# Row normalisation on one core: every load and store as one DMA with one descriptor per partition

## The chip, the cores and the metric

One Trainium2 chip, of which one core runs the program. The core has compute engines (DVE, the vector engine; ACT, the scalar engine; POOL; PE, the matrix engine, unused here), a synchronisation engine SP that here issues loads, and 16 DMA engines that move data between HBM, where the inputs and outputs lie, and the on-chip memory of 128 partitions. The metric is the device time of one execution in microseconds, lower is better.

## The reference

```python
def setup_inputs():
    batch, seq, dim = 32, 512, 1024
    return {"x": np.random.randn(batch, seq, dim).astype(np.float32)}

def reference(x):
    sums = np.sum(np.abs(x), axis=-1, keepdims=True)
    return (x / (sums + 1e-8)).astype(np.float32)
```

Each of the 16,384 rows of 1,024 float32 values is divided by the sum of its absolute values. 67.11 MB are read and 67.11 MB written.

## The kernel before

The 16,384 rows are dealt out to 128 partitions, 128 rows to each, and cut into 11 tiles: ten of 12 rows per partition (48 KB per partition, 6,144 KB in all) and a last one of 8 rows (32 KB per partition, 4,096 KB in all). `piece` says which rows of HBM a tile stands for. Tiles 0, 1 and 10 share a head region of 32 rows per partition, so that in HBM a partition's part of such a tile lies 128 KB from the next partition's; tiles 2 to 9 are contiguous blocks. Within a tile one partition's rows are always one contiguous run in HBM and in the on-chip memory.

Four tile buffers (`BUFS = 4`) hold a tile each, and the result is written over the input in place. The order is written by hand: loads 0 to 3 are issued by SP at the start; then for each tile its compute, its store, and the load of the tile four places on, which goes into the buffer that the store has just emptied. Load i+4 therefore waits on SP until store i has landed in HBM. Loads are issued on SP's DMA queue (q1 in the profile), stores on ACT's (q10); both queues feed the same 16 DMA engines, each of which serves 8 of the 128 partitions.

The compute of a tile (`normalize`): DVE sums the absolute values of all rows in one reduction (L47), adds the epsilon (L54) and takes the reciprocal (L56). The rows are then multiplied: the first `kv` rows by one DVE instruction (L58), the next `kt` rows one by one on DVE (L65), the last ones one by one on ACT (L68). `split` gives `(kt, ks)` by tile; for tile 0 it is `(3, 4)`: five rows in L58, three in L65, four on ACT. For tiles 3 to 8 DVE does all rows in L58.

How a transfer is cut into descriptors is set by `max_dma_last_dim`, the most bytes that one descriptor may move; one descriptor is one packet in the profile's count. `HALF` is 24,576 B, half a partition's part of a full tile, `WHOLE` is 49,152 B, all of it. Loads 0 and 1 go out whole (one descriptor per partition), all later loads in halves (L87); the last load, of 32 KB per partition, becomes two of 16 KB. Store 0 is two DMAs: its first three rows (`FIRST = 3`) in descriptors of one row, 4 KB, then nine rows in one descriptor of 36 KB. Stores 1 to 7 are one DMA with two descriptors per partition; store 8 (`last - 2`) is two DMAs of six rows, 24 KB each; stores 9 and 10 are one DMA with one descriptor per partition (L97).

Of the kernel before, what the change touches and what calls it, by code (L numbers as in the profile page):

```python
# [1 line left out]

# [4 lines left out]

FP32 = mybir.dt.float32
EPS = 1e-8


@with_exitstack
def kernel(
    ctx: ExitStack,
    tc: tile.TileContext,
    x: bass.AP,
    out: bass.AP,
):
    nc = tc.nc
    P = nc.NUM_PARTITIONS  # L20

    x_flat = x.flatten_outer_dims()
    out_flat = out.flatten_outer_dims()
    n, d = x_flat.shape

    R = 12
    BUFS = 4
    HEAD = 32
    per_partition = n // P
    assert n % P == 0 and (per_partition - HEAD) % R == 0  # L30
    rows = [R] * ((per_partition - HEAD) // R + 2) + [HEAD - 2 * R]

    def piece(flat, i):
        head = flat[: P * HEAD, :].rearrange("(p r) d -> p r d", p=P)
        if i < 2:
            return head[:, R * i : R * (i + 1), :]
        if i == len(rows) - 1:
            return head[:, 2 * R :, :]
        a = P * (HEAD + R * (i - 2))
        return flat[a : a + P * R, :].rearrange("(p r) d -> p r d", p=P)  # L40

    sbuf = ctx.enter_context(tc.tile_pool(name="sbuf", bufs=BUFS))
    stats = ctx.enter_context(tc.tile_pool(name="stats", bufs=len(rows)))

    def normalize(x_tile, k, kv, kt):
        s = stats.tile([P, R], FP32)
        nc.vector.tensor_reduce(  # L47
            out=s[:, :k],
            in_=x_tile[:, :k, :],
            axis=mybir.AxisListType.X,  # L50
            op=mybir.AluOpType.add,
            apply_absolute_value=True,
        )
        nc.vector.tensor_scalar_add(out=s[:, :k], in0=s[:, :k], scalar1=EPS)  # L54
        inv = stats.tile([P, R], FP32)
        nc.vector.reciprocal(out=inv[:, :k], in_=s[:, :k])  # L56
        if kv:
            nc.vector.tensor_mul(  # L58
                out=x_tile[:, :kv, :],
                in0=x_tile[:, :kv, :],  # L60
                in1=inv[:, :kv].unsqueeze(2).to_broadcast([P, kv, d]),
            )
        for r in range(kv, kv + kt):
            row = x_tile[:, r, :]
            nc.vector.tensor_scalar_mul(out=row, in0=row, scalar1=inv[:, r : r + 1])  # L65
        for r in range(kv + kt, k):
            row = x_tile[:, r, :]
            nc.scalar.activation(  # L68
                out=row,
                in_=row,  # L70
                func=mybir.ActivationFunctionType.Copy,
                scale=inv[:, r : r + 1],
            )

    last = len(rows) - 1
    split = {0: (3, 4), 1: (0, 3), 2: (0, 3), last - 1: (0, 2), last: (4, 4)}

    tiles = {}

    HALF, WHOLE = 24576, 49152
    FIRST = 3

    def load(i):
        x_tile = tiles[i] = sbuf.tile([P, R, d], FP32, name="x_tile")
        nc.sync.dma_start(out=x_tile[:, : rows[i], :], in_=piece(x_flat, i), max_dma_last_dim=WHOLE if i < 2 else HALF)  # L87

    def store(i):
        if i == 0:  # L90
            parts = [(0, FIRST, 4 * d), (FIRST, R, WHOLE)]
        elif i == last - 2:
            parts = [(0, R // 2, HALF), (R // 2, R, HALF)]
        else:
            parts = [(0, rows[i], WHOLE if i >= last - 1 else HALF)]
        for a, b, size in parts:
            nc.scalar.dma_start(  # L97
                out=piece(out_flat, i)[:, a:b, :],
                in_=tiles[i][:, a:b, :],
                max_dma_last_dim=size,  # L100
            )

    def compute(i):
        k = rows[i]
        kt, ks = split.get(i, (0, 0))
        normalize(tiles[i], k, k - kt - ks, kt)

    with tc.manual_schedule():
        for i in range(BUFS):
            load(i)  # L110
        for i in range(len(rows)):
            compute(i)
            store(i)
            if i + BUFS < len(rows):
                load(i + BUFS)


# [1 line left out]
_INS = ['x']  # L119
_OUTS = [((32, 512, 1024), 'float32')]  # L120


# [23 lines left out]
```

## Time and profile before

| what | value |
|---|---|
| median of 3 runs | 316.5 us (316.41 to 316.51) |
| span of the profiled execution, first to last instruction | 315.2 us |
| time of the profiled execution beyond its span | not given by the profile; the median is 1.3 us above the span |
| HBM read and written | 67.11 MB each, 426 GB/s over the span |
| DVE: reductions (L47), 11 | 138.2 us |
| DVE: broadcast multiplications (L58), 10 | 113.6 us |
| ACT: row multiplications (L68), 16 | 17.2 us |
| DMA issues | 11 loads (SP), 13 stores (ACT) |
| loads of 6,144 KB, issue to landing, median | 36.9 us |
| stores of 6,144 KB, issue to landing, median | 49.1 us |

The span runs from the first to the last instruction. Busy time of an engine is given as time and share of the span; issuing a DMA is not counted as busy time, so the issuing queues appear as SPq and ACTq. A row of instructions ends with the idle time just before it in brackets and what ended it. For DMA queues the profile counts packets, MB and the share of the time of all 16 engines that the packets took. A small packet of 4 bytes that marks the completion of a DMA on an engine is counted as well.

### The profile page before, as it was taken

The numbers are of one execution on the slowest core, as the hardware profiler recorded it, in microseconds if no ns is written. First come the engines' busy times: TensorE is split into PE (matmuls) and PEld (weight loads), VectorE is DVE, ScalarE is ACT, GpSimd is POOL, SyncE is SP. The second block draws the span as 40 slices with busy tenths as digits, with TensorE's granted clock in tenths as the row PEclk, the third lists the DMA queues.
The fourth block names the chain that finished last, engine by engine and source line by source line (L and its number), as shares of the span: only waits on it lengthen the run. The fifth ranks groups of instructions, "written<-read, shape, count | busy, mean of one in ns | idle before, by whom it ended". The sixth has DMA issues, their size and how long they took to land.

```text
span 315.2 us, 172 instructions
## 1 busy us (share of the span) xinstructions
DVE 260.6 (83%) x50; ACT 18.5 (6%) x17; POOL 0.2 (0%) x4
## 2 busy tenths in 40 slices
DVE  0079999999999999989996997999699969999000
ACT  0010503004000000000000000000000000203200
POOL 0000000000000000000000000000000000000000
DMA  8999999999999999999999999999999999999997
GB/s 318 480 399 412 437 407 464 411 436 413 415 446 437 415 446 437 415 449 434 415 449 437 412 449 437 412 449 437 415 446 437 415 437 434 432 428 496 399 408 324
DMA packets 5761, 134.22 MB, mean 426 GB/s; under 512 B 385, under 2 KB 385, under 8 KB 769
## 3 DMA queue, kind: packets, MB, share of 16 engines
q1 hardware_dynamic: 2736, 67.11, 49.8%
q10 hardware_dynamic: 3024, 67.11, 49.4%
q14 instruction: 1, 0.00, 0.0%
HBM read 67.11 MB, written 67.11 MB: 426 GB/s over the span
## 4 chain that ended last, share of the span: by engine, by line
DVE 40%; DMA 33%; another core or an unknown queue 18%; ACT 1%; issue 0%; SPq 0%
DVE s L47 23%; DMA x_tile<-in_x_dram 17%; DMA out_dram<-x_tile 16%; DVE x_tile L58 15%; ACT x_tile L68 1%; DVE x_tile L65 1%; DVE inv L56 0%; DVE s L54 0%; SPq L87 0%
## 5 line engine op out<-in xcount | busy, mean ns | idle before, releaser
L47 DVE TENSOR_REDUCE s<-x_tile 128x12 f32<-128x12288 f32 (+1 forms) x11 | 138.2, 12562 | 29.8 <-DMA x_tile<-in_x_dram 29.8
L58 DVE TENSOR_TENSOR x_tile<-x_tile,inv 128x12288 f32<-128x12288 f32 (+3 forms) x10 | 113.6, 11358 | 0.5
L68 ACT ACTIVATE x_tile<-x_tile,inv 128x1024 f32<-128x1024 f32 x16 | 17.2, 1138 | 256.9 <-DVE inv L56 256.9
L65 DVE TENSOR_SCALAR x_tile<-x_tile,inv 128x1024 f32<-128x1024 f32 x7 | 4.8, 749 | 0.0
L56 DVE RECIPROCAL inv<-s 128x12 f32<-128x12 f32 (+1 forms) x11 | 2.5, 226 | 0.4
L68 ACT ACT_TABLE_LOAD x1 | 1.3, 1283 | 17.8 <-DMA x_tile<-in_x_dram 17.8
L54 DVE TENSOR_SCALAR s<-s 128x12 f32<-128x12 f32 (+1 forms) x11 | 1.9, 174 | 0.4
L130 POOL MEMSET const-bfloat16-1.0<- 128x1 bf16 x1 | 0.1, 101 | 0.0
L130 POOL MEMSET const-uint8-127<- 128x1 uint8 x1 | 0.1, 101 | 0.0
L130 POOL MEMSET const-float32-0.0<- 128x1 f32 x1 | 0.1, 98 | 0.2 <-issue 0.2
L130 POOL MEMSET const-float32-1.0<- 128x1 f32 x1 | 0.1, 98 | 0.0
## 6 DMA issues: line engine op xcount, KB each, us to landing
x_tile<-in_x_dram SPq DMA_DIRECT2D x10, 6144.0 KB, 36.9
out_dram<-x_tile ACTq DMA_DIRECT2D x8, 6144.0 KB, 49.1
out_dram<-x_tile ACTq DMA_DIRECT2D x2, 3072.0 KB, 33.4
out_dram<-x_tile ACTq DMA_DIRECT2D x1, 4608.0 KB, 37.9
x_tile<-in_x_dram SPq DMA_DIRECT2D x1, 4096.0 KB, 32.2
out_dram<-x_tile ACTq DMA_DIRECT2D x1, 4096.0 KB, 20.9
out_dram<-x_tile ACTq DMA_DIRECT2D x1, 1536.0 KB, 29.3
```

Of the source, the lines that this page charges most:

```text
L47: nc.vector.tensor_reduce(out=s[:, :k], in_=x_tile[:, :k, :], axis=mybir.AxisListType.X, op=mybir.AluOpType.add, apply_absolute_value=True,)
L54: nc.vector.tensor_scalar_add(out=s[:, :k], in0=s[:, :k], scalar1=EPS)
L56: nc.vector.reciprocal(out=inv[:, :k], in_=s[:, :k])
L58: nc.vector.tensor_mul(out=x_tile[:, :kv, :], in0=x_tile[:, :kv, :], in1=inv[:, :kv].unsqueeze(2).to_broadcast([P, kv, d]),)
L65: nc.vector.tensor_scalar_mul(out=row, in0=row, scalar1=inv[:, r : r + 1])
L68: nc.scalar.activation(out=row, in_=row, func=mybir.ActivationFunctionType.Copy, scale=inv[:, r : r + 1],)
L130: nc = _bacc.Bacc("TRN2", target_bir_lowering=False, num_devices=1)
```

## The change

All loads and stores are issued without `max_dma_last_dim`. One partition's part of a tile is a contiguous run, and so each load and each store becomes one DMA with one descriptor per partition: 48 KB for tiles 0 to 9, 32 KB for tile 10. Store 0 is no longer cut into its first three rows and the rest, and store 8 no longer into two halves. The compute, the four buffers, the order of issue and the queues are the same.

```diff
-    HALF, WHOLE = 24576, 49152
-    FIRST = 3
-
     def load(i):
         x_tile = tiles[i] = sbuf.tile([P, R, d], FP32, name="x_tile")
-        nc.sync.dma_start(out=x_tile[:, : rows[i], :], in_=piece(x_flat, i), max_dma_last_dim=WHOLE if i < 2 else HALF)
+        nc.sync.dma_start(out=x_tile[:, : rows[i], :], in_=piece(x_flat, i))
 
     def store(i):
-        if i == 0:
-            parts = [(0, FIRST, 4 * d), (FIRST, R, WHOLE)]
-        elif i == last - 2:
-            parts = [(0, R // 2, HALF), (R // 2, R, HALF)]
-        else:
-            parts = [(0, rows[i], WHOLE if i >= last - 1 else HALF)]
-        for a, b, size in parts:
-            nc.scalar.dma_start(
-                out=piece(out_flat, i)[:, a:b, :],
-                in_=tiles[i][:, a:b, :],
-                max_dma_last_dim=size,
-            )
+        nc.scalar.dma_start(out=piece(out_flat, i), in_=tiles[i][:, : rows[i], :])
```

## The prediction

> **What bounds the kernel now.** I read the page first: the engine rows, the slices and the queues.
>
> ```profile
> span 315.2 us, 172 instructions
> DVE 260.6 (83%) x50; ACT 18.5 (6%) x17; POOL 0.2 (0%) x4
> ...
> DMA  8999999999999999999999999999999999999997
> ...
> q1 hardware_dynamic: 2736, 67.11, 49.8%
> q10 hardware_dynamic: 3024, 67.11, 49.4%
> ```
>
> The 16 DMA engines are busy in every slice and their two queues together fill 99.2% of the span; DVE, the busiest compute engine, fills 83%. So the end is set by the sum of what the DMA engines must do, unless some order of the work leaves them with nothing to do. q1 carries the loads (issued by SP), q10 the stores (issued by ACT). Next I read the busy time by stretches:
>
> ```profile
> 40.00:50.00 10.00, 10.00 (x1) 0.00 (x0) 0.00 (x0) 1.00 1.00 424
> 50.00:60.00 10.00, 9.90 (x4) 3.23 (x3) 0.00 (x0) 1.00 0.97 414
> ...
> 86.00:96.00 10.00, 10.00 (x1) 0.00 (x0) 0.00 (x0) 1.00 1.00 433
> ...
> 160.00:189.10 29.10, 26.34 (x5) 0.00 (x0) 0.00 (x0) 1.00 1.00 432
> ...
> 289.00:313.30 24.30, 2.70 (x4) 4.22 (x4) 0.00 (x0) 1.00 1.00 432
> ```
>
> The last column is GB/s. The rate is 432 to 433 where loads and stores of 24 KB packets mix and where only stores of 48 and 32 KB are left; it is lower only from 40 to 60 us, where the first store's 4 KB packets run. Third, the DMA view of two stretches, 41 to 62 us (first pair) and 77 to 80 us (last line), packets and MB by queue:
>
> ```profile
> q1 hardware_dynamic: 323, 7.54, 83.7%
> q10 hardware_dynamic: 322, 1.32, 15.2%
> ...
> x_tile<-in_x_dram SPq DMA_DIRECT2D x1, 6144.0 KB, 33.2
> ```
>
> Packets are as many in both queues while bytes stand 6 to 1: an engine takes one packet (one descriptor's record) from each queue in turn, whatever its size. And load 4, issued at 76.8 us into an empty q1, lands after 33.2 us. Fourth, the timeline gives the rhythm and the tail:
>
> ```profile
> 168.21 12.95 DVE L47 TENSOR_REDUCE s<-x_tile 128x12 f32<-128x12288 f32 x1 [2.60 <-DMA x_tile<-in_x_dram]
> ...
> 197.29 12.95 DVE L47 TENSOR_REDUCE s<-x_tile 128x12 f32<-128x12288 f32 x1 [2.62 <-DMA x_tile<-in_x_dram]
> ...
> 279.85 0.34 ACTq L97 DMA_DIRECT2D out_dram<-x_tile  x1
> ...
> 293.25 0.34 ACTq L97 DMA_DIRECT2D out_dram<-x_tile  x1
> ```
>
> Each reduction starts when its load lands, every 29.08 us. In that time an engine moves 16 load and 16 store packets of 24,576 B: 0.909 us each. Load 4 thus came 33.2 - 29.1 = 4.1 us late: about 1.0 us from issue to a first packet (load 0: issue 0.73, first packet record 1.74) and 3.4 packets of the other queue already taken up.
>
> **The packets that go.** Each engine serves 8 of the 128 partitions. Packets per engine before: loads 2 x 8 whole, 8 x 16 half and 16 in the last tile, 160; stores 8 x (3 + 1) for tile 0, 7 x 16, 16 for tile 8, 8 and 8 for the last two, 176. Together 336, and 16 x 336 plus 24 DMAs x 16 completion records is 5760, the page's 2736 + 3024. After: 22 DMAs x 8 = 176. So 160 packets per engine go, the bytes stay. The price of one: in the packet records two starts on one engine lie 908 ns apart for 24,576 B and 1812 ns for 49,152 B; 2 x 908.3 - 1811.8 = 4.8 ns is saved by joining two. 4,096 B take 155 ns, which gives 4.7 ns beside the same rate. 160 x 4.7 ns = 0.75 us. By the recorded durations (912 and 1815 ns, which overlap a little) it is 9 ns and 1.4 us; if joining saved nothing, 0. I take 0.75, since starts on a busy engine are what adds up to the end.
>
> **The first store.** Load 0 lands at 17.8. If the engines then ran at their steady rate, load 1 (8 x 1.812 = 14.5), loads 2 and 3 (32 half packets, 29.1) and store 0 (8 x (3 x 0.155 + 1.360) = 14.6) would be done at 17.8 + 58.2 = 76.0. The second part of store 0, issued at 38.8 (the two issues together last from 36.78 to 39.18), lands 37.9 us later: 76.7. So 0.7 us are lost here, where the table shows 424 and 414; the packet records show it as load packets of up to 1.6 us instead of 0.91 beside 4 KB stores, up to 65 us, and hardly any after that. After the change no 4 KB packet exists and every mix is of large packets. Bounds: 0 (the loss belongs to the first mixing of the queues, whatever the size) and -0.7. The nearest row is the mix of equal large packets (433 and 432 GB/s, no slow packet), so I take -0.7.
>
> Its first rows now wait for the rest of the tile: ACT issues at 38.8 instead of 36.8, behind DVE's three row multiplications. Cost nothing: q1 has loads 2 and 3 queued, so no engine idles; behind it on ACT stands only tile 1's work at 52.1. Two issues (0.4 us each) vanish from ACT, which is idle 256.9 us: nothing. SP's queue is the same 11 issues in the same order, each behind the landing of the store four tiles earlier.
>
> **What moves, and whether it stays covered.** A newly filled queue now waits behind larger packets: 1.0 + 3.4 x 1.812 = 7.2 us. Store 0 begins at 38.8 + 7.2 = 46.0, just as load 2 is through; load 3 and store 0 then alternate 16 packets and both land near 17.8 + 4 x 14.5 = 75.8. Load 4 is issued there, begins at 83.0, and with 15 packets in turn (27.2) and 0.9 to the landing (before: 80.9 + 31 x 0.909 = 109.1, landed 110.0) is there at about 111.1, where DVE comes free (111.2 before). From then on 16 x 1.812 = 28.99 us a tile: load 9 lands at 256.1 (255.5 before), store 9 is issued at 279.85 + 0.6 = 280.5. Load 10 (8 x (1.21 + 1.81) = 24.2) lands at 280.3, store 10 is issued near 294. The engines, meanwhile, are to finish at about 312.3 (their last packet ends at 313.8 before, less the 1.45 us summed below), so store 9's packets begin at 312.3 - 8 x 1.21 - 8 x 1.81 = 288.1 and it has 288.1 - 280.5 - 1.0 = 6.6 us to spare (before: store 9, issued 279.85, landed after 24.6; 304.45 less 14.5 and 0.5 is 289.5, so 8.6). Loads up to 6.6 us later cost nothing; beyond that each microsecond is one at the end.
>
> **Sum.** -0.75 - 0.7 = -1.45 us on a span of 315.2: 313.7. The profile gives no time for its execution beyond the span; the runs' median of 316.5 is 1.3 above it, which I leave as it is: 315.05, given as 315.1 us (-0.45%).
>
> **Rivals.**
> 1. Only packets are saved; the 0.7 us come again where 48 KB stores first meet loads. For it: the slow packets sit at the start and at the end of the first mix. Against: the mixes from 81 us on begin without any. 316.5 - 0.75 = 315.75.
> 2. No change: the saving is eaten or the joint packet is not cheaper in a mix, which no row of 48 KB beside 48 KB shows. 316.5.
> 3. Slower, mixed large packets: a load packet waits for its data when a packet of 48 KB stands before it. A row for such a wait is the 4 KB mix, where a load packet takes 938 ns on average from its start to the next instead of 908. 30 ns on the 64 load packets of tiles 3 to 10 is +1.9 us: 316.5 - 0.75 + 1.9 = 317.65. It outweighs the saving from 12 ns a packet on and is measurably slower from 22. Against it: the 24 KB mix shows none, nor does the last load's mix of 16 KB with 24 KB.
> 4. Slower, the tail runs dry: if a new queue waits for more than 3.4 packets, load 4 and every later load come later, DVE follows, and past 6.6 us (from 7 packets on) the engines idle between stores 8 and 9. At 9 packets load 4 is 5.6 x 1.81 = 10.1 us later than reckoned, 3.5 us past the slack: 318.6; each packet more is 1.8 us more. Against it: 33.2 us for load 4, and 323 packets beside 322. The Trainium skill (DMA: Bandwidth & Descriptors, Queues, rings and completion order) has this rule: an engine drains about 9 to 17 descriptors from one queue before it turns to the next. By that rule the trace does not agree: turns here are of one descriptor, and load 4's 4.1 us leave room for three or four.
>
> **How the numbers follow.** No change means within 0.2%, 315.87 to 317.13, about what a measurement of this kernel can tell. Forecast 0.38, rival 1 0.17, rival 2 0.17, rival 3 0.20, rival 4 0.08. Faster: 0.37 of the forecast and 0.11 of rival 1, 0.48. Same: the rest of these two, 0.07, 0.15 of rival 2 and 0.02 of rival 3, 0.24. Slower: 0.18 of rival 3, 0.08 and 0.02 of rival 2, 0.28. The forecast's own range is 314.4 (the packets at 9 ns) to 315.7. With both signs in play the range of eight in ten goes from 314.4 to 317.9, just past rival 3.
>
> **What would show it.** q1 and q10 with 1584 packets each; reductions 29.0 us apart from tile 5 to 9; store 0 landing near 76 and load 4 about 35 us after its issue; 432 GB/s or more from 45 to 75 us (a dip there is rival 1); a rhythm above 29.1 us is rival 3; a slice with idle DMA after 280 us is rival 4. Store 10 issued at 294 with DMA busy to the end would bear out that the order of loads is covered. The forecast is wrong if the rhythm does not shorten, or if it does and the span does not.

## The result, and the profile after

The change makes the kernel slower, by 0.4%: 317.61 us median (316.97 to 320.25, 13 executions) against 316.58 us (316.38 to 316.73, 13 executions) of the kernel before, ratio 1.0041, 95% interval 1.0025 to 1.0057. It also makes it uneven: before's executions lie within 0.35 us of each other, the changed kernel's within 3.3.

The profiled execution of the changed kernel is one of the shortest, 316.97 us with a span of 315.0. Its page, the engine rows, the slices and the queues:

```profile
span 315.0 us, 168 instructions
DVE 260.5 (83%) x50; ACT 18.5 (6%) x17; POOL 0.2 (0%) x4
...
DMA  8999999999999999999999999999999999999997
...
q1 hardware_dynamic: 1584, 67.11, 49.8%
q10 hardware_dynamic: 1584, 67.11, 49.2%
```

1584 packets in each queue, as the descriptors say, and the DMA engines as busy as before. The timeline, for the rhythm and the two last stores:

```profile
169.17 12.95 DVE L47 TENSOR_REDUCE s<-x_tile 128x12 f32<-128x12288 f32 x1 [2.53 <-DMA x_tile<-in_x_dram]
...
198.17 12.95 DVE L47 TENSOR_REDUCE s<-x_tile 128x12 f32<-128x12288 f32 x1 [2.53 <-DMA x_tile<-in_x_dram]
...
280.53 0.34 ACTq L85 DMA_DIRECT2D out_dram<-x_tile  x1
...
293.82 0.34 ACTq L85 DMA_DIRECT2D out_dram<-x_tile  x1
```

Loads land every 29.00 us (29.08 before). Store 9 is issued at 280.53, store 10 at 293.82. Now the DMA view of two stretches, 38.8 to 46 us (first line) and 120 to 149 us (the pair); columns are packets, MB, share of the time of 16 engines:

```profile
q1 hardware_dynamic: 39, 1.92, 79.3%
...
q1 hardware_dynamic: 144, 6.29, 50.1%
q10 hardware_dynamic: 144, 6.29, 50.1%
```

In the steady mix both queues have 144 packets, 128 of data and 16 small completions: 0.501 x 29 us x 16 / 128 = 1.816 us a packet, the price of 48 KB. From 38.8 to 46 us, where the first store begins, 39 load packets take 0.793 x 7.2 x 16 = 91.4 us, 2.34 us each, on average half a microsecond too much; in the packet records the excess stands in one or two load packets of each engine, where its first store packet comes. The busy time by stretches (last column GB/s) shows the same place:

```profile
40.00:50.00 10.00, 10.00 (x1) 0.00 (x0) 0.00 (x0) 1.00 1.04 393
50.00:60.00 10.00, 9.90 (x4) 3.23 (x3) 0.00 (x0) 1.00 0.99 428
...
160.00:189.10 29.10, 26.41 (x5) 0.00 (x0) 0.00 (x0) 1.00 1.00 434
```

393 GB/s where before had 424. Large packets make a ten-microsecond figure coarse (a packet counts where it starts); added up from the packet records, the time beyond the usual duration is 1.29 us per engine here, all of it between 40 and 47 us. Before it was 0.67 us, and most of it stood elsewhere: 0.1 us from 38 to 50 us, beside the first 4 KB store packets, and over 0.5 us from 62 to 65 us, in the last two packets of load 3. The DMA view of before from 62 to 64.5 us has these 32 load packets:

```profile
q1 hardware_dynamic: 32, 0.79, 95.2%
```

0.952 x 2.5 x 16 / 32 = 1.19 us each instead of 0.91. In the changed kernel no load packet is late there. So one stall has gone, and a larger one has come at another place.

So this execution shows a saving in the mix and a loss at its start. It does not show why the median is 1 us above before. The spans of all executions, which are listed beside their times, say more:

| kernel | spans, us | median | time beyond the span |
|---|---|---|---|
| before, 32 executions beside the later runs | 314.8 to 315.3 | 315.0 | 1.63 |
| changed, the 13 above | 315.0 to 318.3 | 315.6 | 1.96 |

Of the 1.03 us, 0.33 lie around the span and the rest, 0.6 to 0.7, in it.

### The profile page after: what moved, and what is told of

It reads as the page before. It is cut to its first block, busy times and chain, and to the rows that moved or that the text cites. A ratio compares the mean times of both kernels' runs of the same rounds, so it can differ in the third digit from the quotient of the medians.

```text
span 315.0 us, 168 instructions
## 1 busy us (share of the span) xinstructions
DVE 260.5 (83%) x50; ACT 18.5 (6%) x17; POOL 0.2 (0%) x4
## 3 DMA queue, kind: packets, MB, share of 16 engines
q1 hardware_dynamic: 1584, 67.11, 49.8%
q10 hardware_dynamic: 1584, 67.11, 49.2%
## 4 chain that ended last, share of the span: by engine, by line
DVE 41%; DMA 33%; another core or an unknown queue 18%; ACT 1%; issue 0%; SPq 0%; DVEq 0%
DVE s L47 23%; DMA x_tile<-in_x_dram 17%; DMA out_dram<-x_tile 16%; DVE x_tile L58 15%; DVE x_tile L65 1%; ACT x_tile L68 1%; DVE inv L56 0%; DVE s L54 0%; SPq L82 0%; DVEq L125 0%
## 6 DMA issues: line engine op xcount, KB each, us to landing
x_tile<-in_x_dram SPq DMA_DIRECT2D x10, 6144.0 KB, 37.6
```

## The experiments

All medians are of executions compared with the kernel before on the same chip. "Late" is what data packets took beyond their usual duration, from the packet records of the one profiled execution of each run, as a mean over the 16 engines. It is nearly all in load packets, except after 70 us: there half of it is in store packets in e5, 0.6 of the 5.0 us in e6, and all in e13. "The first mix" is the time up to 70 us, without the first packets of load 0.

| run | what differs | median, us | spans, us | late in the first mix, us | late after 70 us, us |
|---|---|---|---|---|---|
| before again (e9) | nothing | 316.58 | 314.9 to 315.1 | 0.63 | 0 |
| changed again (e4) | nothing from after | 317.55 | 314.7 to 317.0 | 1.12 | 0 |
| changed, third (e12) | nothing from after | 317.34 | 314.9 to 315.7 | 1.20 | 0.08 |
| e1 | after, store 0 as before | 319.33 | 314.8 to 319.3 | 0.72 | 0.18 |
| e2 | before, store 0 whole | 317.59 | 315.3 to 316.0 | 1.09 | 0 |
| e3 | after, store 0 in 24 KB | 318.32 | 315.9 to 317.3 | 0.87 | 0.27 |
| e5 | before, stores 1 to 8 whole | 322.97 | 319.8 to 323.3 | 0.57 | 0.60 |
| e6 | before, all loads whole | 323.85 | 321.4 to 324.0 | 0.73 | 5.02 |
| e7 | after, four small instructions more | 317.47 | 315.2 to 316.2 | 1.33 | 0.07 |
| e8 | before, store 0 all in 4 KB | 317.25 | 315.1 to 316.1 | 0.65 | 0.07 |
| e10 | copy in 48 KB | 317.09 | 314.8 to 317.3 | 1.27 | 0.12 |
| e11 | copy in 24 KB | 317.23 | 315.3 to 315.8 | 0.96 | 0 |
| e13 | before, mix in 16 KB | 317.67 | 315.7 to 316.2 | 0.73 | 0.05 |

**Where is the loss: at the first store or in the mix? (e1 to e4)** e1 gives the changed kernel before's first store; e2 gives the kernel before the changed first store; e3 cuts the first store in two 24 KB descriptors.

```diff
 # e1, after:
     def store(i):
+        if i == 0:
+            for lo, hi, size in [(0, 3, 4 * d), (3, R, 49152)]:
+                nc.scalar.dma_start(
+                    out=piece(out_flat, i)[:, lo:hi, :],
+                    in_=tiles[i][:, lo:hi, :],
+                    max_dma_last_dim=size,
+                )
+            return
         nc.scalar.dma_start(out=piece(out_flat, i), in_=tiles[i][:, : rows[i], :])
 # e2, before:
-            parts = [(0, FIRST, 4 * d), (FIRST, R, WHOLE)]
+            parts = [(0, R, WHOLE)]
```

> The changed kernel with store 0 cut as before (three rows in 4 KB, nine in 36 KB); all else in one descriptor per partition. Theory A (the loss is made where the first large store packets meet the loads; large packets elsewhere are cheaper): the stall of 1.3 us a DMA engine near 40 us goes and about 0.6 us near 62 us comes in its place, the span is 314.3 to 314.8 us, and the executions lie within 0.5 us of each other as before's do. Theory B (large packets make the stalls wherever loads and stores mix): executions spread over 1 us or more like the changed kernel's, median span 315.5 or more.

> The kernel before with store 0 alone sent whole, in one DMA of 48 KB descriptors; all others as before. Theory A: the stall near 40 us is there and varies, median span 315.5 to 316.5 us, executions spread by 1 us or more. Theory B: no spread, span 315.2 us or a little less.

> The changed kernel with store 0 in two descriptors of 24 KB per partition. Theory A, if the size of the first store's packets sets the stall: between the whole first store and the one in 4 KB rows, about 0.7 us lost near 40 us, span about 314.5 us. Theory A, if any packet much above 4 KB does it: the same stall and spread as with 48 KB. Theory B: as the changed kernel, 315.0 to 316 us.

> The changed kernel again, for a second profiled execution and its spread. Theory A: whatever its span is above 313.8 us stands as slow load packets between 40 and 47 us. Theory B: slow packets in other stretches too. Both: the time is about 1.95 us above the span, as in the runs so far, against 1.36 us for the profiled execution before, if that gap belongs to the program and not to the execution.

Both theories hold for a part. The first store alone, sent whole (e2), costs 1.0 us (ratio 1.0033, interval 1.0021 to 1.0045; 0.33 of it around the span). Its DMA view from 38.8 to 46 us has the same stall with load packets of 24 KB:

```profile
q1 hardware_dynamic: 77, 1.89, 76.0%
```

0.760 x 7.2 x 16 / 77 = 1.14 us instead of 0.91 for each. The stall near 40 us is 0.03 to 0.17 us per engine with 4 KB store packets first (0.5 to 0.7 us come near 60 us instead), 0.87 with 24 KB (one profile, e3) and 1.1 to 1.3 with 48 KB. The spread that theory A expected of e2, 1 us or more, is not there (0.6 us in five executions). But without the stall near 40 us e1 is the worse kernel: 319.33 us, spans spread over 4.5 us. Its only difference from before is the size in the mix (and store 8 in one DMA). Theory A expected 314.3 to 314.8 us here; only the shortest, 314.8, is there. The two changes don't add up: the first store alone costs 1.0 us, the large packets in the mix alone (e1) 2.7, both together again 1.0, and with a first store in 24 KB (e3) 1.7. No run shows why a larger first store goes with a smaller loss later. e4, the changed kernel again, fits theory A in its profiled execution, a short one: 1.12 us near 40 us, nothing later, span 314.8. The profiled execution of e3, 317.3 us long, shows what happens. First its timeline, where the reductions start as loads land:

```profile
138.74 12.95 DVE L47 TENSOR_REDUCE s<-x_tile 128x12 f32<-128x12288 f32 x1 [1.00 <-DMA x_tile<-in_x_dram]
167.75 12.95 DVE L47 TENSOR_REDUCE s<-x_tile 128x12 f32<-128x12288 f32 x1 [2.54 <-DMA x_tile<-in_x_dram]
197.05 12.95 DVE L47 TENSOR_REDUCE s<-x_tile 128x12 f32<-128x12288 f32 x1 [2.83 <-DMA x_tile<-in_x_dram]
226.41 12.95 DVE L47 TENSOR_REDUCE s<-x_tile 128x12 f32<-128x12288 f32 x1 [2.94 <-DMA x_tile<-in_x_dram]
255.86 12.95 DVE L47 TENSOR_REDUCE s<-x_tile 128x12 f32<-128x12288 f32 x1 [3.04 <-DMA x_tile<-in_x_dram]
```

The rhythm is 29.01, then 29.30, 29.36 and 29.45 us. Then the end of its busy time by stretches, whose last but one column is the share of the DMA engines:

```profile
290.00:313.00 23.00, 3.15 (x7) 4.27 (x4) 0.00 (x0) 1.00 0.98 423
313.20:316.10 2.90, 0.00 (x0) 0.00 (x0) 0.00 (x0) 1.00 0.05 23
```

After 313.2 us 5% of the DMA time is used, less than one engine in 16. In the completions, 15 engines have finished store 10 at 314.1 us and the last one at 316.4; for load 4 they were within 0.4 us of each other. A load has landed when its slowest engine is done, and that one engine lost 0.15 to 0.73 us in each of eight single packets, six of them of loads, from 130 us on.

**Which side's packets, and what surrounds them? (e5 to e8)** e5 takes stores 1 to 8 whole and leaves the loads in halves, e6 the other way round. e8 cuts all of store 0 into 4 KB rows. e7 adds instructions to the changed kernel and leaves its transfers alone.

```diff
 # e5, before:
-        elif i == last - 2:
-            parts = [(0, R // 2, HALF), (R // 2, R, HALF)]
         else:
-            parts = [(0, rows[i], WHOLE if i >= last - 1 else HALF)]
+            parts = [(0, rows[i], WHOLE)]
 # e6, before:
-..., max_dma_last_dim=WHOLE if i < 2 else HALF)
+..., max_dma_last_dim=WHOLE)
 # e7, after:
     with tc.manual_schedule():
+        pad = stats.tile([P, R], FP32, name="pad")
+        nc.vector.memset(pad[:, :], 0.0)
+        for r in range(3):
+            nc.scalar.activation(
+                out=pad[:, r + 1 : r + 2],
+                in_=pad[:, r : r + 1],
+                func=mybir.ActivationFunctionType.Copy,
+            )
 # e8, before:
-            parts = [(0, FIRST, 4 * d), (FIRST, R, WHOLE)]
+            parts = [(0, FIRST, 4 * d), (FIRST, R, 4 * d)]
```

> The kernel before with stores 1 to 8 in one descriptor of 48 KB per partition; loads and store 0 as before. Theory C (single DMA engines fall behind when the load packets in the mix are 48 KB): executions lie within 0.5 us of each other as before's do, all 16 completions of a late transfer within 0.8 us, span 314.8 to 315.0 us. Rival D (it is the size of the store packets): one engine's completions fall 1 to 3 us behind in most executions, spread of the times 1 us or more.

> The kernel before with all loads in one descriptor per partition; stores as before. Theory C: one engine falls behind, times spread over 1 us or more above 316.3 us. Rival D: no spread, span 314.8 to 315.0 us.

> The changed kernel with one small memset on DVE and three copies of one column on ACT added while both wait for load 0; nothing of the transfers is changed. If the time around the span (1.96 us here, 1.36 us before, 1.64 us with the first store cut) follows the number of instructions in the engines' programs, it falls to about 1.36 to 1.64 us with the span as the changed kernel's. If it follows the DMAs, it stays at 1.96 us.

> The kernel before with all 12 rows of store 0 in 4 KB descriptors. If the stall of 0.5 us at 62 us is the arrival of the first large store packet, it goes or moves to where store 1's 24 KB packets meet load 4, and the span changes by +0.3 us (72 packets more at 4.7 ns) less 0.5 us at best: 315.0 us. If the stall belongs to the end of load 3, whatever stands beside it, it stays and the span is 315.5 us.

e5 and e6 missed both theories by far, 2% slower each, because I had left out what the profile had already shown: one packet from each queue in turn means that unequal packets share the bytes unequally. The DMA view of e5 from 150 to 170 us, then its busy time by stretches near the end, then its timeline:

```profile
q10 hardware_dynamic: 111, 5.46, 63.1%
q1 hardware_dynamic: 129, 3.17, 37.1%
```

```profile
280.00:289.00 9.00, 8.90 (x4) 2.19 (x2) 0.00 (x0) 1.00 0.89 384
289.00:296.00 7.00, 6.98 (x2) 0.00 (x0) 0.00 (x0) 1.00 0.58 248
```

```profile
293.14 0.34 ACTq L95 DMA_DIRECT2D out_dram<-x_tile  x1
...
306.54 0.34 ACTq L95 DMA_DIRECT2D out_dram<-x_tile  x1
```

Loads get about a third of the bytes, so each lands late, DVE follows, store 9 is issued at 293.14 instead of 279.85 us, and from 289 to 296 us the engines are idle for 42% of the time, 2.9 us. That is rival 4's dry tail, brought about by another cause. In e6 the loads get the greater share while both queues have work, nothing runs dry, but the packets are late by 5.0 us per engine, 4.4 of it in load packets, on all engines. One thing e5 does show, and theory C had it the other way: its load packets are of 24 KB, and still one engine's completions come up to 3.0 us after the other fifteen (load 8: 236.4 and 239.4 us). So large load packets are not needed for a late engine. More these two don't tell; both change the balance as well.

e7 moves the time around the span from 1.96 to 1.65 us with the same transfers. It is a matter of the program: before has 1.63, the copies 1.78, each constant to about 0.1 us over its executions. Of the kernels that compute, all with store 0 in two DMAs have a mean of 1.60 to 1.65 (before, e1, e5, e6, e8, e13), and those with it in one have 1.95 to 1.97 (changed, e2, e3) unless instructions are added (e7). Which instruction decides it was not tried.

e8 keeps the stall at 62 us (0.5 us) though no large store packet comes there, and its span of 315.5 us is what was expected for that case. The stall stands at the last one or two packets of load 3, when nothing is queued behind them; the arrival of a large store packet is not needed for it. Nor is the end of load 3, as e13 below shows, where load 3 goes on to 76 us. Its DMA view from 57.5 to 60 us:

```profile
q1 hardware_dynamic: 32, 0.52, 74.4%
```

0.744 x 2.5 x 16 / 32 = 0.93 us for each load packet of 16 KB instead of 0.61, right before the first store packet of 36 KB. What the profiles have in common is this: the stall stands right before the stores first take a third or more of an engine's bytes, be it by large packets beside the loads (changed, e2, e3, e13) or because the loads end (e1, e6, e8). Beside 4 KB packets they take a fifth at most. That is a reading of these traces; no run was made to test it.

**Does computing have a part in it? (e9 to e12)** The copies replace the computation by one addition to one column; the sums and the multiplications are left out. e11 adds `max_dma_last_dim=24576` to every load and store.

```diff
     def compute(i):
-        k = rows[i]
-        kt, ks = split.get(i, (0, 0))
-        normalize(tiles[i], k, k - kt - ks, kt)
+        col = tiles[i][:, : rows[i], 0:1]
+        nc.vector.tensor_scalar_add(out=col, in0=col, scalar1=EPS)
```

> The kernel before again, for the spans of several executions beside their times. If the time around the span belongs to the program, it is 1.36 us in each and the span 315.1 to 315.3 us; if it differs from launch to launch, it lies anywhere from 1.36 to 1.97 us.

> The changed kernel without its computation: DVE only adds to one column of each tile, so that loads and stores mix from 18 us on with the engines never waiting for compute; the sums and multiplications are left out. Theory C2 (large packets of equal size let single DMA engines fall behind in the mix, whatever the compute engines do): spread of the times of 1 us or more and completions of one engine 1 to 3 us behind, median above that of the copy in 24 KB. Rival E (the engines fall behind because DVE and ACT use the on-chip memory at the same time): no spread, and about 0.8 us less than the copy in 24 KB (176 packets per engine fewer at 4.7 ns).

> The same copy with every load and store in descriptors of 24 KB (the last tile's in 16 KB). Theory C2 and rival E alike: executions within 0.5 us of each other, all 16 completions within 0.8 us.

> The changed kernel a third time. Theory C2: if the profiled execution has a span above 315.5 us, one or a few engines' completions are behind the others by what it has above 314.8 us, from the steady stretch on; if it has 315 us or less, no engine is behind. Rival F (all its loss is the stall of all engines near 40 us, whose size varies): the completions stay together and that stall is larger by the difference.

e9 gives before's time around the span as 1.63 us in each execution. It is constant, as expected for the program, but not the 1.36 expected, which came from a span and a time of different executions.

The copy in 48 KB spreads over 2.5 us (316.61 to 319.09), the copy in 24 KB over 0.5. In the profiled 48 KB copy one engine ends its last packet at 314.8 us and the other fifteen at 313.0 to 313.7; in the 24 KB copy all end between 313.5 and 314.1 (half-way its completions lie 2 us apart, more than the 0.8 expected, but no packet is late there). So rival E falls: DVE and ACT do nearly nothing here and an engine still falls behind. The mean engine of the 48 KB copy is done at 313.36 us, of the other at 313.79: the 176 packets fewer (0.83 us) less what it is later in stalls (0.4) are in the sum. The median, 0.14 us lower for 48 KB, is within the noise of the two, and the expectation that it would be above the 24 KB copy's was wrong.

e12 (315.4 us) fits rival F more than C2: no engine falls behind in the steady stretch. Four engines end 0.7 to 1.0 us after the others; all four had a longer stall near 40 us (1.6 to 1.8 us) and lost 0.24 to 0.35 us in the last load.

**Long executions of the changed kernel itself, and smaller packets (e13 to e16).** e13 sets `HALF` to 16384 and sends store 8 as one DMA; e14 to e16 are one execution each of the changed kernel.

> The kernel before with the mix in 16 KB instead of 24 KB (loads 2 to 9 and stores 1 to 8 in three descriptors per partition; store 8 one DMA). Theory C2 (single engines fall behind only with large packets; a packet costs 4.7 ns): no later stall, executions within 0.5 us of each other, 128 packets per engine more, so the span is 0.6 us above before's 314.95: about 315.5 us. Rival G (any change of the packet sizes brings stragglers): spread of 1 us or more.

> The changed kernel, one look. Theory C2: if the span is above 316 us, one engine's last store ends by that difference after the others and the share of busy DMA engines in the last microseconds is about one sixteenth; if it is about 315 us, only the stall near 40 us is there.

> As the look before it: above 316 us a single late engine, at about 315 us none.

> As the look before it: above 316 us a single late engine, at about 315 us none.

e14 to e16 had spans of 315.8, 316.3 and 315.6 us. The longest, e15, in its timeline:

```profile
140.59 12.95 DVE L47 TENSOR_REDUCE s<-x_tile 128x12 f32<-128x12288 f32 x1 [2.89 <-DMA x_tile<-in_x_dram]
169.59 12.95 DVE L47 TENSOR_REDUCE s<-x_tile 128x12 f32<-128x12288 f32 x1 [2.52 <-DMA x_tile<-in_x_dram]
198.98 12.95 DVE L47 TENSOR_REDUCE s<-x_tile 128x12 f32<-128x12288 f32 x1 [2.91 <-DMA x_tile<-in_x_dram]
228.28 12.95 DVE L47 TENSOR_REDUCE s<-x_tile 128x12 f32<-128x12288 f32 x1 [2.89 <-DMA x_tile<-in_x_dram]
257.90 12.95 DVE L47 TENSOR_REDUCE s<-x_tile 128x12 f32<-128x12288 f32 x1 [3.20 <-DMA x_tile<-in_x_dram]
```

Beside the steady 29.00 us there are steps of 29.39, 29.30 and 29.62. Here all engines are late, by about 0.8 us each after 70 us, in the early packets of the loads (near 116, 174, 205 and 234 us), and two engines end 1 us after the rest. So the expectation of a single late engine above 316 us was too narrow: what this long execution loses, it loses in load packets of the mix, in all engines. e14 and e16 show another picture, that of e12, and perhaps the commoner one, since 31 of the 36 executions of the changed kernel have spans below 316.3 us. The rhythm is steady, the stall near 40 us is 1.21 and 1.26 us on average, but three engines were stalled for 1.8 to 1.9 us there, and two of them then lost 0.4 to 0.7 us in a packet of the last load, near 273 us. These two end 1.2 to 1.5 us after the mean of the rest.

e13's executions lie within 0.55 us, with almost nothing late after 70 us (one engine, 0.6 us, in two store packets). Its span is 1.0 us above before's; 0.6 was expected for 128 packets more. The mean engine, done at 314.17 us, is 0.7 to 0.8 us behind before's (313.33 and 313.50 in its two profiles), near the expectation; the rest is its one late engine.

## Why the prediction was wrong

The forecast was 315.1 us, 1.4 us faster than before; the kernel came out 1.0 us slower. The step that failed first is the term of the first store, -0.7 us, which has the wrong sign. Two more terms failed: the loss in the mix of 48 KB beside 48 KB, which was put at nothing, and the time around the span, which was taken as 1.3 us.

**The packets that go: right.** The mechanism and its size held. 160 packets fewer, 4.7 ns each, show as a rhythm of 29.00 us; the shortest executions of the changed kernel have a span of 314.7 us although their start is slower. The mean engine bears out the sum: in e4 it is done at 313.19 us, in e9 (before) at 313.33, 0.14 earlier; 0.75 less for the packets, 0.49 more in the first mix and 0.11 more in the very first packets make 0.15.

**The first store: this term has the wrong sign.** I took -0.7 us, on the ground that every mix of equal large packets in the trace of before was free of slow packets. That row was of a mix already running. I also placed the loss wrongly: the rows of 424 and 414 GB/s from 40 to 60 us have little to do with it, since over 0.5 of the 0.67 us stands from 62 to 65 us. That part did go, as forecast. What I had not reckoned with is a new stall of 1.1 to 1.3 us near 40 us, where the first 48 KB store packets come. Rival 1 had the place, with 0.7 us instead. The term was about +0.55 instead of -0.7, an error of 1.25 us. e2 shows it alone. Together with the packets this gives 314.95 - 0.75 + 0.5 = 314.7 us, just what the changed kernel's best executions have (e4's profile: 314.8).

**The mix of 48 KB beside 48 KB: a loss that was put at 0, and not as rival 3 had it.** I said that no row showed it and put the loss at 0. In most executions there is a loss beyond the mean stall. It is not 30 ns on each packet, as rival 3 had it, but 0.1 to 0.7 us in a few load packets, on one or more engines and not in every execution. Spread through the mix it shows in one profile of the changed kernel (e15), and in e1, e3 and the copy; in e12, e14 and e16, nearer the median, it is the uneven first stall and the last load. The sum of a mean engine misses this, since a transfer lands with its slowest engine. From the best span to the median it is 315.6 - 314.7 = 0.9 us, unevenness of the first stall included; in the longest execution 3.6 us. That the measured 317.61 us lies in the range, and beside rival 3's 317.65, is luck: the sign of rival 3, a rhythm above 29.1 us, is absent (29.00), and the 938 ns that it was priced by is an average over the stall at 62 us; up to 62 us a load packet in that mix takes 913 ns from its start to the next. The Trainium skill (Perfetto Trace Analysis, What "DMA-bound" means) says that for a kernel bound by its DMA engines large descriptors are what matter; beyond 24 KB the runs here do not agree, 314.8 to 319.3 us of span for e1 against 314.8 to 315.3 for before.

**Span and time.** I added 1.3 us to the span, the difference between a profiled execution and the median of others. In all executions listed with both, before's gap is 1.63 us, so a span of 315.2 goes with a time of about 316.8, and the changed program's gap is 1.96 us. This step costs 0.66 us of the miss, 0.33 of it as a real difference between the kernels. e7 shows that it depends on the program: there the transfers are the same.

**The order of the work: right in the main.** Load 4 was reckoned to land at 111.1 us and did at 111.1; load 9 at 256.1, and the reduction started at 256.17; stores 9 and 10 at 280.5 and 294, and came at 280.53 and 293.82. Within the first mix I was off: load 3 and store 0 land at 82.2 and 73.4 us instead of both near 75.8; nothing waits for load 3 before 84.8 us. Load 4 is issued when store 0 lands, earlier than reckoned, and takes 37.6 us instead of about 35, so that the two errors cancel; that its landing was right to 0.1 us is luck. The tail never runs dry, so rival 4 did not come about here; e5 shows that a dry tail is real. The Trainium skill's rule named there, turns of 9 to 17 descriptors, does not agree with the trace after the change either: 144 packets beside 144 in 29 us, and in the packet records the queues change over one by one, with two packets of a queue in a row about once per tile.

Adding up against the forecast of 315.05: 1.25 us (first store), 0.9 (uneven and late engines) and 0.66 (around the span), less 0.2 because the shown span was 0.2 above the usual 314.95, make 2.6; measured 317.61 - 315.05 = 2.56. The 0.9 is itself the difference of two measured spans, so that the sum closes is no test of it.

Why a load packet waits at the start of a mix, or later with large packets, was not settled. Computing is not needed for it (e10). The size of the packets in the mix matters: with 16 or 24 KB on both sides the executions of one kernel lie within 0.2 to 1.1 us of each other (the most in e8), with 48 KB on both sides within 0.85 to 4.5. Whether it is the load's or the store's packet was not separated; e5 shows only that it need not be the load's.

## What to carry to other kernels

Where the DMA engines are the bound, fewer descriptors are worth only their fixed cost (4.7 ns here), while the size of those that mix sets how loads and stores share the engines: keep both equal, and check the spread of executions and not only one trace. A transfer lands with its slowest engine, so a mean over 16 engines can look better (313.36 us in the 48 KB copy, 313.79 in the 24 KB one) while single executions get longer (up to 319.09 against 317.55). For a price at the start of a phase, take no row from its steady part, and compare a span with the time of the same execution.

## What the runs showed of the hardware

A DMA engine takes one descriptor from each queue in turn whatever its size, and so store packets of twice the size took 63% of the bytes (5.46 against 3.17 MB in 20 us) and made the kernel 2% slower. Past the first packets of a run, loads alone and stores alone run without late packets at 48 KB; loads beside stores do so, after the first mix, in both profiles of before with 24 KB (432 GB/s), and only in some executions with 48 KB (434 GB/s in the best). The first mix of the two directions costs the engines 0.6 to 1.3 us each, once, and in the traces here it does so right before the stores first take a third or more of the bytes. And the time around the same work differs by 0.3 us with a few instructions that nothing waits for (1.96 and 1.65 us).
